# Residual of six tiles and attended half of four tiles: added by GpSimd's accumulating transfers in place of VectorE

## The chip, the cores and the metric

The kernel runs on one core of one Trainium2 chip. Its five engines are TensorE (PE; its weight loads are shown apart as PEld), VectorE (DVE), ScalarE (ACT), GpSimd (POOL) and SyncE (SP). Each works through its own list of instructions in order and waits on semaphores where it needs another engine or a transfer. Transfers between main memory and the on-chip memory (SBUF) are issued from an engine's queue and carried by 16 DMA engines. Matmul results are written to PSUM. The metric is the time of one execution in microseconds on the device.

## The reference

One layer of a bidirectional encoder, float32, S = 1024 tokens, width D = 1024, feed-forward width 2816:

```python
x = x + 0.5 * post1(FFN1(pre1(x)))
h = pre2(x); z = h @ w_in
x = x + post2(concat(attn, rwkv) @ w_out)     # h1 -> h2
x = x + 0.5 * post3(FFN2(pre3(x)))
```

`pre` and `post` are RMS norms with a gain. FFN is `(silu(h @ w_gate) * (h @ w_up)) @ w_down`. `attn` is a dilated attention of 8 heads (512 columns), `rwkv` a two-way RWKV-7 scan of 8 heads (512 columns). The change lies in the third line and in `pre3`. There, for each token, with `y` the concatenated 1024 columns:

```python
o  = y @ w_out
h2 = h1 + o / rms(o) * gain_post2
f  = h2 / rms(h2) * gain_pre3          # input of FFN2
```

## The kernel before, in words

The 1024 tokens are eight tiles of 128 rows, worked off in the order 2, 3, 4, 5 (half 0) and 0, 1, 6, 7 (half 1) of the token blocks. I call the tiles t0 to t7 in this working order. A row tile is 128 partitions by 1024 columns, 512 KB. In the rows of the instruction order below, t0 to t3 are `row_16320` to `row_16323`, and t4 to t7 are `row_16316` to `row_16319`.

Products are float32 made of two parts: every operand is split into a high part (ScalarE copy, L186) and a remainder (VectorE subtraction, L187), and a product is three matmuls (high x high, high x low, low x high). The feed-forward products use seven products for eight blocks (class `_GateUp`, n from 1 to 7). For this the weights' slabs and the rows are added and subtracted beforehand: the slabs by VectorE at L60 to L63, the rows by GpSimd in `factor_sums` (L339 to L343).

The stage of interest lies between the end of the RWKV part and FFN2. The attended part's product with its half of `w_out` was computed earlier and lies in main memory (`hp_d`). Then, for each tile, in `out_project` and `done`:

1. The tile's rows of `hp_d` are loaded into the row tile (SyncE).
2. For each 512 columns: 12 matmuls (L1064) of the RWKV half with `w_out` into a PSUM buffer `pw`, of which there are two, and a VectorE addition of `pw` to the row (L1095).
3. `post`: load of the tile's rows of `h1_d` into `res` (one buffer, SyncE, L182); sum of squares on ScalarE (L244), root (L245), reciprocal on VectorE (L246); the gain on VectorE (L256); the residual addition on VectorE (L257); store of the row to `h2_d` (SyncE, L258).
4. For the tile before: `pre`, that is the same three steps of the norm (L244 to L246) and the gain on VectorE (L266), in place in the row, so after the store of this tile. For tiles of half 1, `factor_sums` follows on GpSimd.
5. For the tile two back: `turn`, TensorE's transposes (L330) and the split of the result (L186, L187), the operand of FFN2's first products.

FFN2's first products (L81) run between these steps; the first slabs of their weights are loaded on GpSimd's queue and later ones on SyncE's (L284). A framework's scheduler fixes each engine's order when the program is built.

The row addition and the store stand in `post` so:

```python
nc.vector.scalar_tensor_tensor(ft, ft, rs, gb, op0=OP.mult, op1=OP.mult)   # L256
nc.vector.tensor_tensor(ft, ft, r, op=OP.add)                              # L257
self.nc.sync.dma_start(store[rows, :], ft)                                 # L258
```

Of the kernel before, what the change touches and what calls it, by code (L numbers as in the profile page):

```python
# [10 lines left out]
F32 = mybir.dt.float32  # L11
F32R = mybir.dt.float32r
AF = mybir.ActivationFunctionType
OP = mybir.AluOpType
# [4 lines left out]
S, D, DFF, INW = 1024, 1024, 2816, 3456  # L19
# [144 lines left out]
class _Kernel:  # L164
# [47 lines left out]
    def rstd(self, p, ss, n, scale, eps, post=1.0):  # L212
        V = self.nc.vector
        rs = p.tile([128, n], F32, name="rs", tag="rs", bufs=2)
        V.tensor_scalar(rs, ss, scale, eps, op0=OP.mult, op1=OP.add)
        self.nc.scalar.activation(rs, rs, AF.Sqrt)
        V.reciprocal(rs, rs)
        if post != 1.0:
            V.tensor_scalar(rs, rs, post, None, op0=OP.mult)
        return rs  # L220
# [25 lines left out]
        V.reciprocal(rs, rs)  # L246
        return rs

    def post(self, p, ft, t, gb, scale, res, store):

        nc = self.nc
        rows = slice(t * 128, (t + 1) * 128)
        r = p.tile([128, D], F32, name="res", tag="res")
        self.load(r, res[rows, :])
        rs = self.inv_rms(p, ft, scale)
        nc.vector.scalar_tensor_tensor(ft, ft, rs, gb, op0=OP.mult, op1=OP.mult)  # L256
        nc.vector.tensor_tensor(ft, ft, r, op=OP.add)  # L257
        self.nc.sync.dma_start(store[rows, :], ft)  # L258

    def pre(self, p, ft, gain=None):  # L260
# [825 lines left out]
    def out_project(self, psum, half, W, x, h2, done):  # L1086
        xh, xl = x[half]
        for i in range(4):
            t, ts = self.order[half * 4 + i], slice(i * 128, (i + 1) * 128)
            self.load(h2[t], self.hp_d[t * 128:(t + 1) * 128, :])  # L1090
            for dh in range(2):
                ps = psum.tile([128, 512], F32, name="pw", tag="d")
                self.out_products(ps, W, dh, xh, xl, ts)
                dst = h2[t][:, dh * 512:(dh + 1) * 512]
                self.nc.vector.tensor_tensor(dst, dst, ps, op=OP.add)  # L1095
            done(half * 4 + i)


# [64 lines left out]
    def run(self):  # L1163
        nc = self.nc
# [4 lines left out]
        with self.top as top:  # L1169
# [8 lines left out]
            with ExitStack() as st:  # L1178
                s_pg = ExitStack()
                pg, pt = self.pool(s_pg, "ps_g", space=PSUM), self.pool(s_pg, "ps_t", 2, space=PSUM)  # L1180
                rows = self.pool(st, "rows1", 8, **R)
# [4 lines left out]
                hand = self.pool(s_h0, "hand0", **R)  # L1186
# [30 lines left out]
                x2, low, ps = [], {}, {}  # L1217
                p = self.pool(st, "ffn1")
                hand = self.pool(st, "hand1")
                gb = self.row_bcast(hand, "ffn1_post_g")  # L1220
                LO = [12, 13, 14]

                def ready(half):
                    for ct in LO:
                        ps[ct, half] = self.product(psum, x2, low[ct], (half,))[0]

                def done(i, f):
                    if not i:
                        x2.extend(self.operand(xp, xp))
                    if i == 6:  # L1230
                        for ct in LO:
                            low[ct] = self.weights(ring, self.io["w_in"][0], INW, ATT + ct * 128, p, ("gh", "gl"), GB)
                    self.hand_over(hand, psum, f, i, natural, gb, 0.5, x0, self.h1_d, self.g2c, x2, ready)

                self.down(p, ring, rows, psum, self.hid_d[0], wd, self.ws_d[0], natural, done)
                x = x2
                vw = self.value_weights(ring)
# [80 lines left out]
            rows = self.pool(s_xn, "rows2", 8)  # L1318
            hr = self.row_tiles(rows)
            h2 = {t: hr[i] for i, t in enumerate(self.order)}  # L1320
# [15 lines left out]
            hand = self.pool(st, "hand2")  # L1336
            gb, late = self.row_bcast(hand, "mix_post_g"), {}
            f = self.factors(f0, None)

            def turn(i):  # L1340
                a, b = hr[i % 4], hr[i % 4 + 4]
                for n in (1, 2) if i < 4 else (3,):
                    self.turn_factor(pg, a, b, n, f, i % 4, "ge", 2)
                if i >= 4:
                    self.factor_sums(a, b, True)
# [4 lines left out]
                    self.factor_sums(hr[i - 4], hr[i])  # L1350

            def done(i):
                self.post(hand, hr[i], self.order[i], gb, 1.0, self.h1_d, self.h2_d)
                if i:
                    ready(i - 1)
                else:
                    late["gain"] = self.row_bcast(hand, "ffn2_pre_g")
                if i > 1:
                    turn(i - 2)

            for half in range(2):
                self.out_project(psum, half, W, x, h2, done)
# [10 lines left out]
            with ExitStack() as st:  # L1373
# [12 lines left out]
                p, hand = self.pool(st, "ffn2"), self.pool(st, "hand3")  # L1386
                gb = self.row_bcast(hand, "ffn2_post_g")
# [48 lines left out]
```

## Time and profile before

| | |
|---|---|
| median of 3 runs | 2369.25 us (2357.99 to 2371.84) |
| profiled execution, its own time | 2369.46 us |
| its span, first to last instruction | 2367.7 us |
| mean granted TensorE clock | 0.960 |
| busy: PE, PEld, DVE, ACT, POOL | 2212.2, 1784.9, 1782.8, 1034.4, 608.7 us |
| the stage of the change | about 1640 to 1752 us of the span |

Times inside the span are microseconds from its first instruction. In rows of the trace, `out<-in` are the program's names without buffer numbers: `row` a row tile, `pw` a PSUM buffer of the out-projection, `res` the residual rows, `d_h` the rows h1 or h2 in main memory, `d_hp` the attended half there, `raw` a slab of weights. "Idle before" is the time that the engine stood still ahead of an instruction, with what released it. The feed-forward products make up most of the span on TensorE; the stage above is about a twentieth of it.

### The profile page before, as it was taken

To read this page: it belongs to the slowest core of one execution; us is meant where nothing else is said; L and a number is where in the kernel's file an instruction comes from. 1 tells how busy PE (TensorE), PEld (TensorE's weight loads), DVE (VectorE), ACT (ScalarE), POOL (GpSimd) and SP (SyncE) were. 2 spreads that over 40 slices of the span, in tenths; PEclk is the share of its full clock that TensorE was granted. 3 is DMA by queue.
4 is the path that set the end of the run, shared out by engine and by line. 5 is a ranking of instruction groups with operands and counts; after the bars stand their busy time and mean duration, and the time that the engine had idled before them with its cause. 6 is when DMAs were issued, how large, how long until landed. Compare 5 with 4: busy or idle time off the path is not lost. (4 is left out here: it accounts for less than half of the span.)

```text
span 2367.7 us, 39507 instructions
## 1 busy us (share of the span) xinstructions
PE 2212.2 (93%) x14532; PEld 1784.9 (75%) x14532; DVE 1782.8 (75%) x2957; ACT 1034.4 (44%) x1958; POOL 608.7 (26%) x732
## 2 busy tenths in 40 slices
PE   6999999999999998999995889988799999999997
PEld 4788888878877676788774767765678888887886
DVE  8899999865676344667568767837889999987565
ACT  4322333354676413666545545445442333235453
POOL 6244443400000010111102242432334344441000
PEclk8999999999999998999996798989989999999999
DMA  5354445486652514322369676577534544447655
GB/s 156 107 174 151 170 146 170 167 266 193 220 185 98 193 42 134 91 81 71 94 161 223 165 183 176 151 208 256 178 95 168 174 167 154 169 153 265 195 188 181
DMA packets 359381, 386.04 MB, mean 163 GB/s; under 512 B 74258, under 2 KB 265618, under 8 KB 359188
## 3 DMA queue, kind: packets, MB, share of 16 engines
q1 hardware_dynamic: 308512, 276.43, 38.8%
q0 software_dynamic: 30320, 94.44, 11.3%
q10 hardware_dynamic: 20356, 12.66, 1.9%
q8 instruction: 114, 1.87, 0.3%
q14 instruction: 79, 0.65, 0.1%
HBM read 257.53 MB, written 125.89 MB: 162 GB/s over the span
## 5 line engine op out<-in xcount | busy, mean ns | idle before, releaser
L186 ACT ACTIVATE wh<-raw 128x512 fp32r<-128x512 f32 (+1 forms) x273 | 167.8, 626 | 264.1 <-DVE raw L62 95.0
L187 DVE TENSOR_TENSOR wl<-raw,wh 128x512 fp32r<-128x512 f32 (+1 forms) x273 | 277.6, 1020 | 3.1 <-ACT wh L186 2.0
L81 PE MATMUL gu<-xh,wh 128*128 128x512 f32 x704 | 277.9, 395 | 0.9 <-ACT xh L186 0.8
L81 PE MATMUL gu<-xl,wh 128*128 128x512 f32 x704 | 276.3, 393 | 0.0
L81 PE MATMUL gu<-xh,wl 128*128 128x512 f32 x704 | 276.2, 392 | 0.0
L415 PE MATMUL pd<-gl,gwh 128*128 128x512 f32 x616 | 240.4, 390 | 3.1 <-DVE gl L187 3.1
L415 PE MATMUL pd<-gh,gwh 128*128 128x512 f32 x616 | 239.6, 390 | 0.5 <-DVE row L86 0.5
L415 PE MATMUL pd<-gh,gwl 128*128 128x512 f32 x616 | 239.7, 389 | 0.0
L86 DVE TENSOR_TENSOR row<-gu,row 128x512 f32<-128x512 f32 x308 | 206.4, 682 | 23.2 <-PE gu L81 22.4
L187 DVE TENSOR_TENSOR gwl<-graw,gwh 128x512 fp32r<-128x512 f32 (+1 forms) x176 | 117.0, 667 | 129.7 <-ACT gwh L186 127.5
L116 POOL DMA_DIRECT2D d_hid<-row x154 | 84.7, 551 | 470.6 <-DVE row L114 444.2
L186 ACT ACTIVATE gwh<-graw 128x512 fp32r<-128x512 f32 (+1 forms) x176 | 101.4, 576 | 190.5 <-PE pd L415 162.2
L81 PEld LDWEIGHTS gu<-xh,wh 128*128 128x128 f32 x704 | 133.9, 190 | 29.5 <-ACT xh L186 2.0
L81 PEld LDWEIGHTS gu<-xl,wh 128*128 128x128 f32 x704 | 133.8, 190 | 27.9
L81 PEld LDWEIGHTS gu<-xh,wl 128*128 128x128 f32 x704 | 133.3, 189 | 27.5
L415 PEld LDWEIGHTS pd<-gl,gwh 128*128 128x128 f32 x616 | 115.6, 188 | 28.5 <-DVE gl L187 4.9
L415 PEld LDWEIGHTS pd<-gh,gwh 128*128 128x128 f32 x616 | 115.5, 188 | 25.6 <-DVE row L86 0.8
L415 PEld LDWEIGHTS pd<-gh,gwl 128*128 128x128 f32 x616 | 115.6, 188 | 23.8
L94 ACT ACTIVATE row<-row 128x512 f32<-128x512 f32 x44 | 27.9, 633 | 223.9 <-DVE row L86 216.4
L187 DVE TENSOR_TENSOR gl<-raw,gh 128x512 fp32r<-128x512 f32 x160 | 112.9, 717 | 15.7 <-ACT gh L186 15.4
L145 POOL TENSOR_TENSOR ws<-ws 128x512 f32<-128x512 f32 x88 | 114.4, 1300 | 1.2
L186 ACT ACTIVATE gh<-raw 128x512 fp32r<-128x512 f32 x160 | 98.0, 621 | 32.2 <-DMA raw<-in_ffn_w_down_dram 21.1
(356 smaller groups left out, 5353.4 us busy)
## 6 DMA issues: line engine op xcount, KB each, us to landing
d_hid<-row POOLq DMA_DIRECT2D x154, 256.0 KB, 2.5
graw<-d_hid SPq DMA_DIRECT2D x132, 256.0 KB, 3.0
raw<-in_ffn_w_gate_dram SPq DMA_DIRECT2D x88, 256.0 KB, 3.1
raw<-in_ffn_w_up_dram SPq DMA_DIRECT2D x88, 256.0 KB, 3.3
ws<-in_ffn_w_down_dram SPq DMA_DIRECT2D x88, 256.0 KB, 4.5
d_ws<-ws POOLq DMA_DIRECT2D x88, 256.0 KB, 2.3
raw<-d_ws SPq DMA_DIRECT2D x88, 256.0 KB, 2.7
raw<-in_ffn_w_down_dram SPq DMA_DIRECT2D x66, 256.0 KB, 3.3
```

The costliest lines, as they stand in the source:

```text
L81: self.K.nc.tensor.matmul(ps, a[:, k, :], b[:, k, :], start=(k == 0 and i == 0), stop=(k == 3 and i == 2))
L86: add = lambda o, x: V.tensor_tensor(o, ps, x, op=OP.add)
L94: A.activation(y[:, 0], y[:, 0], AF.Silu)
L116: put = lambda n, y: G.dma_start(self.hid[n - 1, j // 2], y)
L145: G.tensor_tensor(o, a, b, op=OP.subtract)
L186: self.nc.scalar.activation(h, src, AF.Copy)
L187: (eng or self.nc.vector).tensor_tensor(l, src, h, op=OP.subtract)
L415: T.matmul(ps[x], a[:, ts], b, start=(m == 0 and k == 0), stop=(m == NM - 1 and k == 2))
```

## The change

In half 0 (t0 to t3) the attended half is no longer loaded ahead. ScalarE copies `pw` into the row (L1104 of the new text, two copies per tile), and then one transfer from GpSimd's queue adds the tile's rows of `hp_d` to the row in SBUF (L1106, `accum_op` add, 512 KB). In half 1 the load and VectorE's additions stay (L1102).

In `post`, for the first six tiles (`fetch`), there is no load into `res`. After the gain (L257, before L256) a transfer from GpSimd's queue adds the tile's rows of `h1_d` to the row (L259), and the store follows (L262, before L258). t6 and t7 keep the load and the addition (L261, before L257). The gain of `pre` is L270, before L266.

So ten accumulating transfers are added on GpSimd's queue and eight copies on ScalarE; eight PSUM additions and six residual additions leave VectorE; four loads of `hp_d` and six of `h1_d` leave SyncE's queue.

```diff
-    def post(self, p, ft, t, gb, scale, res, store):
+    def post(self, p, ft, t, gb, scale, res, store, fetch=False):
...
-        r = p.tile([128, D], F32, name="res", tag="res")
-        self.load(r, res[rows, :])
+        if not fetch:
+            r = p.tile([128, D], F32, name="res", tag="res")
+            self.load(r, res[rows, :])
         rs = self.inv_rms(p, ft, scale)
         nc.vector.scalar_tensor_tensor(ft, ft, rs, gb, op0=OP.mult, op1=OP.mult)
-        nc.vector.tensor_tensor(ft, ft, r, op=OP.add)
+        if fetch:
+            nc.gpsimd.dma_start(ft, res[rows, :], accum_op=OP.add)
+        else:
+            nc.vector.tensor_tensor(ft, ft, r, op=OP.add)
         self.nc.sync.dma_start(store[rows, :], ft)
...
-            self.load(h2[t], self.hp_d[t * 128:(t + 1) * 128, :])
+            src = self.hp_d[t * 128:(t + 1) * 128, :]
+            if half:
+                self.load(h2[t], src)
             for dh in range(2):
                 ps = psum.tile([128, 512], F32, name="pw", tag="d")
                 self.out_products(ps, W, dh, xh, xl, ts)
                 dst = h2[t][:, dh * 512:(dh + 1) * 512]
-                self.nc.vector.tensor_tensor(dst, dst, ps, op=OP.add)
+                if half:
+                    self.nc.vector.tensor_tensor(dst, dst, ps, op=OP.add)
+                else:
+                    self.nc.scalar.copy(dst, ps)
+            if not half:
+                self.nc.gpsimd.dma_start(h2[t], src, accum_op=OP.add)
             done(half * 4 + i)
...
-                self.post(hand, hr[i], self.order[i], gb, 1.0, self.h1_d, self.h2_d)
+                self.post(hand, hr[i], self.order[i], gb, 1.0, self.h1_d, self.h2_d, i < 6)
```

The scheduler's order on the engines around the change follows, before and after, at three places. `junk` takes the squares that the sum is made of, `rs1` is the norm's factor, `wh` and `xh` are high parts and `wl` and `xl` remainders of weights and of the transposed rows.

First the start of the stage on ScalarE, before: the norms of t0 and t1, slab halves, the pre norm of t0, the norm of t2, and the first transposed rows.

```order
L244 ACTIVATE junk_16645,rs1_16646<-row_16320 128x1024
L245 ACTIVATE rs1_16646<-rs1_16646,eps0_69 128x1
L244 ACTIVATE junk_16686,rs1_16687<-row_16321 128x1024
L245 ACTIVATE rs1_16687<-rs1_16687,eps0_69 128x1
L186 ACTIVATE wh_16587<-raw_16585 128x512
L186 ACTIVATE wh_16593<-raw_16591 128x512
L186 ACTIVATE wh_16599<-raw_16597 128x512
L244 ACTIVATE junk_16694,rs1_16695<-row_16320 128x1024
L245 ACTIVATE rs1_16695<-rs1_16695,eps0_69 128x1
```

After, on ScalarE, from the norm of t1 to the norm of t2:

```order
L244 ACTIVATE junk_16682,rs1_16683<-row_16321 128x1024
L1104 COPY row_16322<-pw_16710 128x512
L245 ACTIVATE rs1_16683<-rs1_16683,eps0_69 128x1
L1104 COPY row_16323<-pw_16753 128x512
L244 ACTIVATE junk_16690,rs1_16691<-row_16320 128x1024
L186 ACTIVATE wh_16599<-raw_16597 128x512
L186 ACTIVATE wh_16605<-raw_16603 128x512
L245 ACTIVATE rs1_16691<-rs1_16691,eps0_69 128x1
L1104 COPY row_16323<-pw_16767 128x512
L244 ACTIVATE junk_16725,rs1_16726<-row_16322 128x1024
```

The last copy of t3 out of PSUM (`pw_16767`) now stands behind the pre norm's square of t0 (`junk_16690`). GpSimd's queue at the same place held four slab loads in a row before; after, it holds them between the transfers:

```order
L1106 DMA row_16320<-d_hp_83 128x1024
L288 DMA raw_16585<-in_ffn2_w_gate_dram 128x4x128
L288 DMA raw_16591<-in_ffn2_w_gate_dram 128x4x128
L1106 DMA row_16321<-d_hp_83 128x1024
L259 DMA row_16320<-d_h1_77 128x1024
L288 DMA raw_16597<-in_ffn2_w_gate_dram 128x4x128
L288 DMA raw_16603<-in_ffn2_w_gate_dram 128x4x128
L1106 DMA row_16322<-d_hp_83 128x1024
L259 DMA row_16321<-d_h1_77 128x1024
L1106 DMA row_16323<-d_hp_83 128x1024
L259 DMA row_16322<-d_h1_77 128x1024
```

Two slab loads have moved behind the residual transfer of t0; the residual transfers of t3, t4 and t5 follow.

Second, the middle of the stage on VectorE, before: the additions for t5 and t6 around the gain of pre of t3 (`b_ffn2_pre_g`) and the gain of post of t5 (`b_mix_post_g`).

```order
L1095 TENSOR_TENSOR row_16318<-row_16318,pw_16939 128x512
L266 SCALAR_TENSOR_TENSOR row_16323<-row_16323,rs1_16858,b_ffn2_pre_g_16653 128x1024
L246 RECIPROCAL rs1_16909<-rs1_16909 128x1
L256 SCALAR_TENSOR_TENSOR row_16317<-row_16317,rs1_16909,b_mix_post_g_16612 128x1024
L257 TENSOR_TENSOR row_16316<-row_16316,res_16847 128x1024
```

After, the same place on VectorE:

```order
L270 SCALAR_TENSOR_TENSOR row_16323<-row_16323,rs1_16848,b_ffn2_pre_g_16651 128x1024
L246 RECIPROCAL rs1_16897<-rs1_16897 128x1
L1102 TENSOR_TENSOR row_16318<-row_16318,pw_16927 128x512
L257 SCALAR_TENSOR_TENSOR row_16317<-row_16317,rs1_16897,b_mix_post_g_16612 128x1024
L187 TENSOR_TENSOR xl0_16310<-pt_16912,xh0_16309 128x4x128
```

The gain of t5 stands behind the gain of pre of t3 in both; the residual addition is gone, and the first addition of t6 has come behind the gain of pre.

Third, the end of the stage on VectorE, before: from the last addition of t7 (`row_16319`). The gain of pre of t7 stands another seven rows below.

```order
L1095 TENSOR_TENSOR row_16319<-row_16319,pw_17009 128x512
L246 RECIPROCAL rs1_16978<-rs1_16978 128x1
L246 RECIPROCAL rs1_17026<-rs1_17026 128x1
L256 SCALAR_TENSOR_TENSOR row_16319<-row_16319,rs1_17026,b_mix_post_g_16612 128x1024
L266 SCALAR_TENSOR_TENSOR row_16317<-row_16317,rs1_16978,b_ffn2_pre_g_16653 128x1024
L257 TENSOR_TENSOR row_16318<-row_16318,res_16967 128x1024
L187 TENSOR_TENSOR xl1_16312<-pt_17041,xh1_16311 128x4x128
L246 RECIPROCAL rs1_17034<-rs1_17034 128x1
L187 TENSOR_TENSOR xl1_16312<-pt_17128,xh1_16311 128x4x128
L266 SCALAR_TENSOR_TENSOR row_16318<-row_16318,rs1_17034,b_ffn2_pre_g_16653 128x1024
L257 TENSOR_TENSOR row_16319<-row_16319,res_17023 128x1024
```

After, on VectorE, from the residual addition of t6 to the gain of pre of t7:

```order
L261 TENSOR_TENSOR row_16318<-row_16318,res_16955 128x1024
L270 SCALAR_TENSOR_TENSOR row_16317<-row_16317,rs1_16966,b_ffn2_pre_g_16651 128x1024
L1102 TENSOR_TENSOR row_16319<-row_16319,pw_16997 128x512
L187 TENSOR_TENSOR xl1_16312<-pt_17029,xh1_16311 128x4x128
L246 RECIPROCAL rs1_17014<-rs1_17014 128x1
L257 SCALAR_TENSOR_TENSOR row_16319<-row_16319,rs1_17014,b_mix_post_g_16612 128x1024
L246 RECIPROCAL rs1_17022<-rs1_17022 128x1
L261 TENSOR_TENSOR row_16319<-row_16319,res_17011 128x1024
L270 SCALAR_TENSOR_TENSOR row_16318<-row_16318,rs1_17022,b_ffn2_pre_g_16651 128x1024
L246 RECIPROCAL rs1_17039<-rs1_17039 128x1
L187 TENSOR_TENSOR xl1_16312<-pt_17072,xh1_16311 128x4x128
L270 SCALAR_TENSOR_TENSOR row_16319<-row_16319,rs1_17039,b_ffn2_pre_g_16651 128x1024
```

The residual addition of t6 and the gain of pre of t5 now stand ahead of the last addition of t7. On SyncE's queue at this end, the load of t7's residual, five loads of FFN2's slabs and then the store of t7 came one after the other before; after, these rows are:

```order
L262 DMA d_h2_80<-row_16318 128x1024
L182 DMA res_17011<-d_h1_77 128x1024
L262 DMA d_h2_80<-row_16319 128x1024
L288 DMA raw_17167<-in_ffn2_w_gate_dram 128x4x128
L288 DMA raw_17169<-in_ffn2_w_gate_dram 128x4x128
L288 DMA raw_17171<-in_ffn2_w_up_dram 128x4x128
```

The store of t7 now stands ahead of these slab loads.

## The prediction

> **What bounds the kernel now.** I read the chain that ended last first, to see which engine sets the end, and then the stage that the diff touches by itself.
>
> ```profile
> PE 26%; DVE 2%; issue 1%; DMA 1%; ACT 0%; POOL 0%; SPq 0%; DVEq 0%; POOLq 0%
> PE gu L81 17%; PE pd L415 9%; DVE row L266 0%; DVE row L257 0%; DMA d_h<-row 0%; DVE row L256 0%; PE pt L330 0%; ACT junk L244 0%; DMA raw<-in_ffn_w_gate_dram 0%; DMA res<-d_h 0%; DVE row L86 0%; POOL row L339 0%; DVE wl L187 0%; POOL row L340 0%; DVE raw L61 0%
> ```
>
> The end hangs on TensorE's products. The lines of this change (L256, L257, L266, the store into d_h) are on the chain, each with under half a per cent. VectorE's busy time over the whole span therefore says little; the stage must be read by itself, in slices of 20 us:
>
> ```profile
> 1640.00:1660.00 20.00, 19.31 (x89) 15.53 (x89) 14.76 (x24) 10.60 (x22) 1.50 (x2) 1.00 0.75 253
> 1660.00:1680.00 20.00, 17.85 (x90) 14.38 (x89) 19.36 (x29) 12.15 (x25) 0.00 (x0) 1.00 0.49 169
> 1680.00:1700.00 20.00, 18.49 (x86) 14.68 (x85) 17.10 (x22) 9.09 (x19) 6.90 (x4) 1.00 0.45 150
> 1700.00:1720.00 20.00, 7.10 (x36) 5.34 (x36) 14.19 (x18) 6.60 (x13) 14.58 (x10) 0.72 0.61 185
> ```
>
> After the slice and its length stand the busy times of PE, PEld, DVE, ACT and POOL, the granted clock, the DMA share and GB/s. Up to 1700 TensorE works 18 to 19 of 20 us with VectorE nearly as full; in the last slice it works 7.1. The chain inside the stage, in order of time:
>
> ```profile
> 1672.00 2.88 DMA d_h<-row
> 1674.97 1.28 DVE row L266
> ...
> 1685.61 3.05 DMA d_h<-row
> 1688.75 1.28 DVE row L266
> ...
> 1694.81 1.16 ACT junk L244 x2
> ...
> 1697.36 0.30 ACT rs L245
> 1697.69 0.17 DVE rs L246
> ...
> 1752.35 147.83 PE gu L81 x652
> ```
>
> VectorE and the store take turns here: the gain of pre (L266) overwrites the row in place, so it waits until the store has read it. Two tiles pass between 1674.97 and 1688.75, 6.9 us each. From 1752.35 on TensorE's work has no gap: the total moves by as much as that point moves.
>
> **What is removed.** Eight PSUM additions and six residual additions leave VectorE:
>
> ```profile
> L1095 DVE TENSOR_TENSOR row<-row,pw x16: 665/675/689, 1640.2 to 1695.3; 128x512 f32<-128x512 f32 x16
> L257 DVE TENSOR_TENSOR row<-row,res x8: 1212/1218/2308, 1656.3 to 1707.7; 128x1024 f32<-128x1024 f32 x8
> DMA to landing us min/median/max: 4.2/4.7/8.3
> ```
>
> That is 8 x 0.675 + 6 x 1.218 = 12.7 us of VectorE, but the stage cannot gain as much, since TensorE is close behind:
>
> ```profile
> 1646.25 0.39 PE L1064 MATMUL pw<-woh,xh 128*128 128x512 f32 x1
> ...
> 1651.71 0.39 PE L1064 MATMUL pw<-woh,xh 128*128 128x512 f32 x1
> ...
> 1703.72 1.03 PE L330 MATMUL pt<-ident,row 128*128 128x128 f32 x8
> ```
>
> Between those two starts lie 24 steps, 5.46 us: the 24 matmuls of one tile. With its eight transposes (1.03) TensorE needs 6.5 us per tile against 6.9 now. The ten loads that leave SyncE's queue were issued ahead of their use; they cost the path nothing, except that `res` has one buffer, which holds up the last tiles (below).
>
> **What is added.** Eight ScalarE copies out of PSUM, and ten accumulating transfers of 512 KB on GpSimd's queue. The copies I price by one of the same size out of PSUM:
>
> ```profile
> L186 ACT ACTIVATE xh<-pt 128x512 fp32r<-128x512 f32 x15 | 8.4, 597 | 21.4 <-PE pt L330 21.4
> ```
>
> 8 x 0.6 = 4.8 us beside 9 to 12 of 20 us of ScalarE's own work: the engine has room, and only their place in its order counts. The accumulates are another matter. What was an addition beside a load issued early becomes a transfer that starts when the row is ready, and the next step waits for its landing. I call the time from issue to landing L. The trace has no such operation; the nearest are these of the window 1636 to 1715, with the median time to landing last:
>
> ```profile
> res<-d_h SPq DMA_DIRECT2D x8, 512.0 KB, 4.7
> d_h<-row SPq DMA_DIRECT2D x8, 512.0 KB, 3.0
> raw<-in_ffn_w_gate_dram POOLq DMA_DIRECT2D x4, 256.0 KB, 4.2
> ```
>
> Lower end of L: a load of the same rows in this stage, median 4.7; the same bytes must come, and the addition might be free. Upper end: the slowest such load, 8.3, and a store of 3.0 behind it, 11.3. I take 4.7 + 3.0 = 7.7, as the row is read, added to and written; for the first two, which fall into the slice with a DMA share of 0.75, I take 8.3, the load that was issued there.
>
> How often does L stand on the path? ScalarE's copy of t3's second half stands behind the square of t0's pre norm, which waits for t0's residual. So the path is: copies of t0; its attended half (L); norm 1.16 + 0.30 + 0.17 = 1.63; gain L257, 1.28; residual (L); on ScalarE the square, two weight halves (priced as the copy) and the root, 1.16 + 2 x 0.60 + 0.30 = 2.66; copy of t3, 0.60; its attended half (L), norm 1.63, gain 1.28, residual (L), store 2.88; L270 of t3, 1.28; gain of t5, 1.28, which stands behind it on VectorE; residual of t5 (L), store 3.05, L270 of t5, 1.28. Behind that stands the last PSUM addition of t7. The fixed parts are 1.63 + 1.28 + 2.66 + 0.60 + 1.63 + 1.28 + 2.88 + 1.28 + 1.28 + 3.05 + 1.28 = 18.9 us, and five L come to 2 x 8.3 + 3 x 7.7 = 39.7. The two weight halves wait for slab loads that GpSimd now issues behind t0's residual; these land in 4.2 us, before the residual does, so they add nothing. Where the path starts and what follows it, by VectorE's and SyncE's rows:
>
> ```profile
> 1645.98 0.69 DVE L1095 TENSOR_TENSOR row<-row,pw 128x512 f32<-128x512 f32 x1 [0.22 <-PE pw L1064]
> ...
> 1650.56 0.69 DVE L1095 TENSOR_TENSOR row<-row,pw 128x512 f32<-128x512 f32 x1
> ...
> 1695.30 0.67 DVE L1095 TENSOR_TENSOR row<-row,pw 128x512 f32<-128x512 f32 x1
> ...
> 1716.01 1.28 DVE L266 SCALAR_TENSOR_TENSOR row<-row,rs,b_ffn_pre_g 128x1024 f32<-128x1024 f32 x1
> 1702.49 1.80 SPq L284 DMA_DIRECT2D raw<-in_ffn_w_gate_dram  x2
> ```
>
> The first is t0's second addition; a copy in its place ends at 1646.6. The second is t1's, begun when its products were done. Then t7's last addition, now at 1695.30, comes at 1646.6 + 18.9 + 39.7 = 1705.2: **9.9 us later**. With L at 4.7 the path gives 1689.0, but TensorE is not there before 1650.5 + 6 x 6.5 = 1689.5, six tiles after t1, so 5.8 us earlier at best. With L at 11.3 it is 1722.0, 26.7 later.
>
> **What comes back behind it.** Today the last L266 starts 20.7 us after t7's addition, since the residual load of t7 waits for the one buffer. With only t6 and t7 loaded, what is left is 0.67 + 1.63 + 1.28 + 1.22 + 3.05 and handovers, some 8.3 us: 12.4 less. But FFN2's first products also wait for its weight slabs, whose loads begin at 1702.49, 7.2 us after that addition; in the new order on SyncE they stand behind t7's store, 0.67 + 1.63 + 1.28 + 1.22 = 4.8 and some 0.7 of handing over and issuing after it, so they come 1.7 earlier. And VectorE, which then builds the sums of these slabs, has t5's L266 (1.28) and t6's residual (1.22) behind it before the last addition. I take 1.7 + 2.5 = **4.2 us back**, between nothing (another load holds the slabs) and 12.4.
>
> Net 9.9 - 4.2 = 5.7 us on the profiled execution's 2369.46: 2375.2, so 2375. That execution is within 0.3 us of the median of the three runs (2369.25), so nothing is to be shifted. The edit breaks even where five L come to 34.0, 6.8 each.
>
> **A rule that speaks against it.** GpSimd issues the transfers while VectorE runs:
>
> ```profile
> 1654.86 0.75 POOL L284 DMA_DIRECT2D raw<-in_ffn_w_gate_dram  x1 [16.09 <-DVE wl L187]
> L116 POOL DMA_DIRECT2D d_hid<-row x154 | 84.7, 551 | 470.6 <-DVE row L114 444.2
> ```
>
> An issue in this stage took 0.75 against a mean of 0.55 over 154 issues in FFN stages where VectorE works too: a fifth of a microsecond more. The Trainium skill's page "SBUF — State Buffer", section "A bandwidth-pool intuition that's wrong (but worth ruling out)", says that a transfer issued by GpSimd can wait until VectorE releases a port that they share, 620 ns alone becoming some 3100. By that rule each of five transfers would take up to 2.5 us more, an estimate from that page; the rows here speak against it.
>
> **The rivals.**
> - An accumulate costs what a load costs (L = 4.7). For it: the addition needs no engine. Against it: reading and writing the row is more than a load does. 5.8 earlier and 4.2 back: 10.0 less, 2359.5. Chance 0.18.
> - Each issue on GpSimd waits for the VectorE operation in progress, at most the longest in the rows above, 2.3 us (L257). Five of these on the path: 11.5 more, 2386.7. The 0.75 row is against it. Chance 0.10.
> - The other side: the accumulate is slow itself, or the 16 engines choke on it. The stage already holds them for 0.75, 0.49 and 0.45 of three slices. One 512 KB copy holds them 1.5 us (524 KB at 169 / 0.49 = 345 GB/s). With the slowest load, the store and one more pass, 8.3 + 3.0 + 1.5 = 12.8, five L are 64.0 and t7's addition 34.2 late; less 4.2, 30.0: 2399.5. It decides from L = 11.5 on, where the loss passes 1% (23.7 us). Then ScalarE's copies wait behind squares, two PSUM buffers stay full, and TensorE starves. Chance 0.22.
> - The change does not do what it says: the order shows the additions gone from VectorE and the transfers on GpSimd, so 0.02.
>
> **How the numbers follow.** My forecast has 0.48. One per cent is about what a measurement of this kernel tells from no change. The range takes the cheap rival's 2359 and the slow one's 2400. Faster by over 1% would need 23.7 us from a stage whose floor gives 5.8 + 12.4: 0.02. Slower by over 1% is the slow rival and a piece of the forecast's upper bound (11.3): 0.24. Within: 0.74.
>
> **What would show it.** Time to landing of the accumulates: near 7.7, or 4.7, or over 11. The last PSUM addition of t7 near 1705, then the last gain of pre about 8 us later. TensorE idle on PSUM buffers released by ScalarE's copies between 1660 and 1700. GpSimd's accumulate issues at 0.55 to 0.75 or above 2. The unbroken L81 stretch beginning near 1758. The forecast is wrong if L is not near 7.7, or if t0's norm is not what holds t3's copy.

## The result, and the profile after

The changed kernel took 2375.94 us, median of 17 runs (2368.25 to 2390.03), beside 2369.25 us for the kernel before in as many runs on the same chip. The ratio is 1.0037 with a 95% interval of 1.0020 to 1.0054: slower by 8.8 us, between 4.7 and 12.8 (the two medians lie 6.7 apart), so clear of no change at all, and inside the 1% that the prediction called no change. Measured again ("the change again" below) it was 1.0041 (1.0015 to 1.0068). The profiled execution after took 2372.87 us, its span is 2370.5 us.

The two spans differ by only 2.8 us, less than the runs do. A part of the program that the change does not touch hides the rest: the last matmul of the attended projection, well ahead of the stage, began some 11 us earlier in the profile after (1552.8 against 1563.8). The granted clock between 1200 and 1400 was 0.85 there instead of 0.80, which I take for the reason. So I compare stages from a mark inside the stage: the second half of t0 leaving PSUM (1645.98 before, by VectorE; 1637.65 after, by ScalarE's copy). From there to the span's end it is 721.7 us before and 732.9 after: 11.1 us more.

The stage in slices of 20 us after, columns as before; on this scale the stage lies 8.3 us earlier than in the slices before (1645.98 less 1637.65), so the slices compare only roughly:

```profile
1640.00:1660.00 20.00, 16.51 (x73) 13.37 (x72) 7.37 (x12) 9.88 (x20) 6.19 (x8) 1.00 1.01 269
1660.00:1680.00 20.00, 13.46 (x59) 10.29 (x58) 9.87 (x17) 9.41 (x20) 2.56 (x3) 0.91 0.96 260
1680.00:1700.00 20.00, 16.91 (x82) 12.97 (x80) 15.04 (x24) 9.97 (x23) 6.45 (x5) 1.00 0.68 155
1700.00:1720.00 20.00, 12.07 (x63) 9.34 (x61) 15.23 (x16) 7.37 (x15) 15.91 (x11) 0.98 0.46 144
```

VectorE is now idle half the time up to 1680 (7.4 and 9.9 of 20 us, 14.8 and 19.4 before), and TensorE with it: 13.5 us where it worked 17.9. The DMA engines are full (1.01 and 0.96; the share adds up the time of all packets, so it can pass 1), at hardly more bytes in the first slice than before (269 against 253 GB/s). In the last slice TensorE does more (12.1 against 7.1).

The ten transfers on GpSimd's queue, by line, with the time from issue to landing below each:

```profile
L259 POOL DMA_DIRECT2D row<-d_h x6: 850/852/877, 1649.4 to 1690.6; - x6
DMA to landing us min/median/max: 6.5/7.4/9.6
L1106 POOL DMA_DIRECT2D row<-d_hp x4: 855/910/967, 1638.5 to 1661.5; - x4
DMA to landing us min/median/max: 7.5/8.3/9.9
```

The path to t7's last addition, by the rows of three engines. First GpSimd (t0's attended half, t0's residual, t3's attended half, then the residuals of t3 and t5):

```profile
1638.55 0.97 POOL L1106 DMA_DIRECT2D row<-d_hp  x1 [9.70 <-ACT row L1104]
...
1649.40 0.88 POOL L259 DMA_DIRECT2D row<-d_h  x1 [3.19 <-DVE row L257]
...
1661.53 0.85 POOL L1106 DMA_DIRECT2D row<-d_hp  x1 [2.69 <-ACT row L1104]
...
1677.44 0.85 POOL L259 DMA_DIRECT2D row<-d_h  x1 [8.25 <-DVE row L257]
...
1690.62 0.85 POOL L259 DMA_DIRECT2D row<-d_h  x1 [5.61 <-DVE row L257]
```

Then, on ScalarE, t0's mark, the squares that wait for the transfers, and the copy of t3 that stands behind the second square:

```profile
1637.65 0.58 ACT L1104 COPY row<-pw 128x512 f32<-128x512 f32 x1
...
1646.11 1.06 ACT L244 ACTIVATE junk<-row 128x1024 f32<-128x1024 f32 x1 [1.12 <-DMA row<-d_hp]
...
1657.53 1.06 ACT L244 ACTIVATE junk<-row 128x1024 f32<-128x1024 f32 x1 [0.90 <-DMA row<-d_h]
...
1660.67 0.57 ACT L1104 COPY row<-pw 128x512 f32<-128x512 f32 x1
...
1671.50 1.06 ACT L244 ACTIVATE junk<-row 128x1024 f32<-128x1024 f32 x1 [2.38 <-DMA row<-d_hp]
```

And VectorE, from t3's gain of post to t7's last addition and its gain of pre:

```profile
1675.63 1.28 DVE L257 SCALAR_TENSOR_TENSOR row<-row,rs,b_mix_post_g 128x1024 f32<-128x1024 f32 x1
...
1687.20 1.27 DVE L270 SCALAR_TENSOR_TENSOR row<-row,rs,b_ffn_pre_g 128x1024 f32<-128x1024 f32 x1
...
1700.94 2.28 DVE L270 SCALAR_TENSOR_TENSOR row<-row,rs,b_ffn_pre_g 128x1024 f32<-128x1024 f32 x1
1703.15 0.67 DVE L1102 TENSOR_TENSOR row<-row,pw 128x512 f32<-128x512 f32 x1
...
1713.90 1.77 DVE L270 SCALAR_TENSOR_TENSOR row<-row,rs,b_ffn_pre_g 128x1024 f32<-128x1024 f32 x1
```

The last two landings of the path, and TensorE's stretch at its end, in the chain that ended last:

```profile
1677.44 6.54 DMA row<-d_h
...
1690.62 6.63 DMA row<-d_h
...
1754.74 24.60 PE gu L81 x108
```

This is the path that the prediction drew. From t0's mark to t7's last addition it takes 1703.15 - 1637.65 = 65.5 us, against 1695.30 - 1645.98 = 49.3 before: 16.2 us later. Behind it the last gain of pre comes after 10.8 us instead of 20.7. TensorE's unbroken stretch begins at 1754.74, that is 117.1 us from the mark against 106.4 before (1752.35): 10.7 us later, nearly all of the 11.1.

### The profile page after: what moved, and what is told of

It reads as the page before. It is cut to its first block, busy times and chain, and to the rows that moved or that the text cites. A ratio compares the mean times of both kernels' runs of the same rounds, so it can differ in the third digit from the quotient of the medians.

```text
span 2370.5 us, 39507 instructions
## 1 busy us (share of the span) xinstructions
PE 2217.0 (94%) x14532; PEld 1788.3 (75%) x14532; DVE 1769.6 (75%) x2943; ACT 1037.4 (44%) x1966; POOL 616.2 (26%) x742
## 5 line engine op out<-in xcount | busy, mean ns | idle before, releaser
L81 PE MATMUL gu<-xh,wh 128*128 128x512 f32 x704 | 277.2, 394 | 2.2 <-ACT wh L186 1.2
L187 DVE TENSOR_TENSOR wl<-raw,wh 128x512 fp32r<-128x512 f32 (+1 forms) x273 | 272.7, 1002 | 4.8 <-ACT wh L186 3.8
L81 PE MATMUL gu<-xh,wl 128*128 128x512 f32 x704 | 275.7, 392 | 0.0
L81 PE MATMUL gu<-xl,wh 128*128 128x512 f32 x704 | 275.6, 392 | 0.0
L81 PEld LDWEIGHTS gu<-xh,wh 128*128 128x128 f32 x704 | 133.4, 190 | 31.5 <-ACT xh L186 2.0
L81 PEld LDWEIGHTS gu<-xl,wh 128*128 128x128 f32 x704 | 133.4, 189 | 27.6
L81 PEld LDWEIGHTS gu<-xh,wl 128*128 128x128 f32 x704 | 133.0, 189 | 27.6
```

Source lines behind the costliest of these rows:

```text
L81: self.K.nc.tensor.matmul(ps, a[:, k, :], b[:, k, :], start=(k == 0 and i == 0), stop=(k == 3 and i == 2))
L187: (eng or self.nc.vector).tensor_tensor(l, src, h, op=OP.subtract)
```

## The experiments

The question was which part costs the 8.8 us, and whether it is landings in series, the load on the DMA engines, or ScalarE's copies. The table gives for each run the ratio to the kernel before with its interval, and from its profile how many of the eight gains of pre VectorE does ahead of t7's last PSUM addition, and three times: from t0's mark to that addition, from there to the last gain of pre, and from t0's mark to the end of the span.

| run | ratio to before | gains ahead | t0 to t7's addition | to the last gain | t0 to the end |
|---|---|---|---|---|---|
| before | 1 | 5 | 49.3 | 20.7 | 721.7 |
| the change | 1.0037 (1.0020 to 1.0054) | 6 | 65.5 | 10.8 | 732.9 |
| the change again | 1.0041 (1.0015 to 1.0068) | 6 | 66.6 | 10.7 | 733.5 |
| residuals alone | 1.0001 (0.9983 to 1.0020) | 6 | 58.4 | 10.7 | 725.1 |
| attended half alone | 1.0055 (1.0035 to 1.0074) | 4 | 55.5 | 27.0 | 736.6 |
| attended half, two residual buffers | 1.0008 (0.9984 to 1.0032) | 5 | 58.9 | 12.4 | 728.1 |
| plain loads | 1.0001 (0.9985 to 1.0017) | 6 | 55.6 | 11.4 | 724.6 |
| copies by VectorE | 1.0054 (1.0031 to 1.0078) | 5 | 63.8 | 14.2 | 735.8 |
| copies alone | 1.0019 (0.9999 to 1.0039) | 4 | 45.9 | 26.7 | 727.4 |
| residuals twice | 1.0131 (1.0102 to 1.0161) | 3 | 65.4 | 34.0 | 752.5 |
| before, two residual buffers | 0.9977 (0.9951 to 1.0003) | 5 | 47.0 | 12.4 | 716.2 |
| the same again | 0.9979 (0.9956 to 1.0003) | 5 | 47.9 | 12.4 | 717.2 |
| and the stores on GpSimd's queue | 1.0010 (0.9991 to 1.0030) | 5 | 51.7 | 14.4 | 721.8 |
| two buffers, residuals added by GpSimd | 1.0003 (0.9979 to 1.0027) | 6 | 54.5 | 10.8 | 723.9 |

A thousandth is 2.4 us. The last column follows the ratios roughly; a single profile, and there is only one of the kernel before, can be off by 4 or 5 us.

The scheduler orders each build anew. Where more gains of pre stand ahead of t7's last addition, that addition comes later and less is left behind it, so the second time and the third are not the same piece of work in every run. Only their sum, from t0's mark to the last gain, can be compared between builds with different numbers of gains ahead: 70.0 us before, 76.3 in the change.

### Residuals alone

The change without its half 0 part: the attended half of all tiles is loaded ahead and added by VectorE.

```diff
-            src = self.hp_d[t * 128:(t + 1) * 128, :]
-            if half:
-                self.load(h2[t], src)
+            self.load(h2[t], self.hp_d[t * 128:(t + 1) * 128, :])
...
-                if half:
-                    self.nc.vector.tensor_tensor(dst, dst, ps, op=OP.add)
-                else:
-                    self.nc.scalar.copy(dst, ps)
-            if not half:
-                self.nc.gpsimd.dma_start(h2[t], src, accum_op=OP.add)
+                self.nc.vector.tensor_tensor(dst, dst, ps, op=OP.add)
```

> Only the six residuals are added by accumulating transfers; the attended half of t0 to t3 is loaded ahead and added by VectorE, as before the change. Theory (transfers in series on the path): from t1's gain only three landings are left before t7's last addition, 3 x 7.4 = 22.2 us, with 15.1 us of stores and gains between them, so that addition comes about 1692 on the scale of the profile before, 3 us earlier than before, and 4 to 5 us more come back behind it: 2361 to 2366 us, faster than before. Rival (every transfer costs its share of the loss, by its traffic): six tenths of 6.7 us, 2373.

It came out level with before; the interval, -4.0 to 4.7 us, takes in the near end of the theory and just the rival. The expected place was wrong: t7's addition came 9.1 us later than before instead of 3 earlier, and 10.0 us less passed behind it; one more gain of pre stands ahead of it than before. The landings were short (median 5.9), but the stores behind two of them were not: in this run's chain

```profile
1647.86 7.34 DMA row<-d_h
...
1655.21 4.90 DMA d_h<-row
...
1669.45 6.17 DMA row<-d_h
...
1675.67 5.88 DMA d_h<-row
```

a store takes 4.9 and 5.9 us, where the prediction's path had 2.88 and 3.05. Six residual transfers cost nothing in sum against the kernel before: from t0's mark to the last gain it is 69.2 us against 70.0. But that kernel waits at its end for its one residual buffer, and this one doesn't.

### The attended half alone

The change without its residual part.

```diff
-                self.post(hand, hr[i], self.order[i], gb, 1.0, self.h1_d, self.h2_d, i < 6)
+                self.post(hand, hr[i], self.order[i], gb, 1.0, self.h1_d, self.h2_d)
```

> Only the attended half of t0 to t3 is added by accumulating transfers behind ScalarE's copies; all eight residuals are loaded and added by VectorE, as before the change. Theory: two landings in series (t1, then t3), and t3's gain of pre comes no later than before, so nothing is lost: 2365 to 2370 us. Rival A (shares by traffic): four tenths of 6.7 us, 2372. Rival B (the loss is TensorE waiting for ScalarE's copies, 7 us in the profile of the change): 2376.

13 us slower (8.3 to 17.5), which is more than the 8.8 (4.7 to 12.8) of the whole change, though the intervals overlap. The theory's "two landings in series" was wrong, as the rows of its GpSimd show:

```profile
1639.18 0.97 POOL L1106 DMA_DIRECT2D row<-d_hp  x1 [9.22 <-ACT row L1104]
...
1645.93 0.92 POOL L1106 DMA_DIRECT2D row<-d_hp  x1 [4.22 <-ACT row L1104]
...
1657.01 0.90 POOL L1106 DMA_DIRECT2D row<-d_hp  x1 [5.06 <-ACT rs L245]
1666.46 0.86 POOL L1106 DMA_DIRECT2D row<-d_hp  x1 [8.54 <-ACT rs L245]
```

and of its ScalarE:

```profile
1664.54 1.06 ACT L244 ACTIVATE junk<-row 128x1024 f32<-128x1024 f32 x1 [4.89 <-DMA row<-d_hp]
...
1665.60 0.56 ACT L1104 COPY row<-pw 128x512 f32<-128x512 f32 x1
```

Each tile's last copy stands on ScalarE behind the square of the tile before, which waits for its landing; so the attended halves of t1, t2 and t3 land one after the other. That makes t7's addition 6.2 us late, although one gain of pre fewer stands ahead of it than before. As much comes on behind it: 27.0 us to the last gain instead of 20.7, with that one gain more to do. The next run asks how much of it is the one buffer. Rival B's 7 us were one wait counted twice, on TensorE (3.5) and on its weight load (3.9).

### The attended half with two residual buffers

Against the change:

```diff
-    def post(self, p, ft, t, gb, scale, res, store, fetch=False):
+    def post(self, p, ft, t, gb, scale, res, store, fetch=False, bufs=1):
...
-            r = p.tile([128, D], F32, name="res", tag="res")
+            r = p.tile([128, D], F32, name="res", tag="res", bufs=bufs)
...
-                self.post(hand, hr[i], self.order[i], gb, 1.0, self.h1_d, self.h2_d, i < 6)
+                self.post(hand, hr[i], self.order[i], gb, 1.0, self.h1_d, self.h2_d, False, 2)
```

> The run with the attended half alone, with two buffers for the residual rows. In that run's profile t7's last addition came 5.0 us later than before, counted from the end of the RWKV stage's last matmul, and the gain of pre of t7 another 6.3 us later behind it. Theory (the 6.3 come from the one residual buffer, whose loads were pushed back in turn): with two buffers the gain of t7 starts 10 to 13 us after its last addition instead of 27, and of the 13 us over before some 5 to 7 remain. Rival (VectorE's or the slabs' work holds the end): 11 to 14 over before, as with one buffer.

Of the 13 us, 1.9 are left (-3.8 to 7.6), and the last gain comes 12.4 us behind t7's addition. The rival is out: the one buffer does hold up the end of the attended half's run. Its residual loads are pushed back tile by tile, each behind the addition of the tile before. The change does not show that loss, as it loads only t6's and t7's residual. But a second buffer also gives the kernel before some 5 us (below), with as many gains ahead and the same 12.4 us. Against that kernel the attended half still costs about 7 us (0 to 14), and its last gain comes 71.3 us from t0's mark instead of 59.4 and 60.2. So the landings have a price of their own here, beside the buffer.

### Plain loads in place of accumulating ones

```diff
-            nc.gpsimd.dma_start(ft, res[rows, :], accum_op=OP.add)
+            nc.gpsimd.dma_start(ft, res[rows, :])
...
-                self.nc.gpsimd.dma_start(h2[t], src, accum_op=OP.add)
+                self.nc.gpsimd.dma_start(h2[t], src)
```

> The ten transfers stay on GpSimd's queue at the same places with the same waits, but are plain loads: they overwrite the row and leave both additions out. Theory (an accumulate takes a load and a write-back, 7.4 to 8.3 us, a plain load 4.7): time to landing of the ten falls to about 5, each of five on the path gives back about 3 us: 2360 us. Rival (the landing is a fixed cost of a transfer on this queue at this place, whether it adds or not): landing stays above 7 us and the time at 2374 to 2376.

Level with before, so 8 to 9 us under the change. The landings are 5.5 (residual) and 5.9 (attended half), not 4.7, so there is no gain over before. By these medians the five landings on the path fall by 2 x 2.4 + 3 x 1.9 = 10.5 us; t7's addition, behind six gains in all three, comes 9.9 and 11.0 us earlier than in the two profiles of the change: the path shortens by what the landings shorten. This is the run that shows the cause: the same transfers at the same places, and without the adding the loss is gone. The residuals' row of this run:

```profile
L259 POOL DMA_DIRECT2D row<-d_h x6: 528/528/549, 1644.3 to 1677.8; - x6
```

The issue itself takes 0.53 us here and 0.85 in the change. What an accumulate takes more, the queue's own share of the 16 DMA engines shows between 1636 and 1720 (packets, MB, share). Before, with four slab loads on this queue:

```profile
q0 software_dynamic: 320, 1.05, 4.6%
```

The change:

```profile
q0 software_dynamic: 1760, 6.29, 39.6%
```

The plain loads:

```profile
q0 software_dynamic: 1760, 6.29, 21.8%
```

For the same packets and bytes, ten transfers take (39.6 - 4.6)% x 84 us = 29.4 us of all engines when they add, and (21.8 - 4.6)% x 84 = 14.4 when they don't: 2.9 us against 1.4 each, twice the time, if the four slab loads take in both what they took before. The Trainium skill's page "Collectives: The Full Stack", section "The bandwidth ceiling: the fold count and why AG ≠ RS ≠ AR", says that the reduce step of a collective runs at half the rate of a copy, since the add needs two source reads. The factor of the transfers here agrees, 2.0; that the second read is the reason, no run here shows.

### Copies by VectorE

```diff
-                    self.nc.scalar.copy(dst, ps)
+                    self.nc.vector.tensor_copy(dst, ps)
```

> All as in the change, but VectorE instead of ScalarE copies the out-projection of t0 to t3 out of PSUM; ScalarE's squares, which wait for the transfers, then no longer stand ahead of these copies. Rival (ScalarE's order is the whole loss): back to the time before, within 2 us. Theory (landings in series, whichever engine holds the copies): behind VectorE's gains the path is still attended half of t1, residual of t1, store, gain of pre of t1, gain of t3, residual of t3, residual of t5, that is four landings of 7.4 to 8.3, and little is gained: 5 to 9 us above before.

12.8 us above before (7.3 to 18.5): not better than the change, and more than expected, though the interval reaches into the 5 to 9. The rival is out: that the copies wait on ScalarE is not the whole loss. On VectorE they wait as well, behind its gains, and in this run's chain the transfer of t3's attended half, issued right behind two others, takes longer to land than any in the change:

```profile
1664.12 13.56 DMA row<-d_hp
```

### Copies alone

The run with the attended half alone, without its four transfers, so the attended half of t0 to t3 is left out.

```diff
-            if not half:
-                self.nc.gpsimd.dma_start(h2[t], src, accum_op=OP.add)
```

> As the run with the attended half alone, but without its four transfers: ScalarE copies the out-projection of t0 to t3 into the rows, nothing is added to it (the attended half of these four tiles is left out), and all residuals are loaded and added by VectorE. Theory (the landings cost, not the copies): before, or up to 4 us faster. Rival (TensorE waits for ScalarE's copies, transfers or not): 8 to 13 us above before, as with the transfers.

4.5 us above before, with an interval that just reaches no change (-0.2 to 9.2): between the two expectations. t7's addition comes 3.4 us earlier, with four gains of pre ahead of it instead of five, and the last gain 26.7 us behind it, as with the transfers; from t0's mark to the last gain it is 72.6 us against 70.0. In SyncE's and VectorE's rows

```profile
1694.34 0.42 SPq L182 DMA_DIRECT2D res<-d_h  x1
1700.12 1.21 DVE L261 TENSOR_TENSOR row<-row,res 128x1024 f32<-128x1024 f32 x1
```

t7's residual is loaded only at 1694.34, 13 us after its last PSUM addition (1680.95), and added when it has landed 5.8 us later. Removing work ahead of the one residual buffer only lengthens the wait for it. Why the end is then later than before, and not equal, stays open. So a part of the attended half's 13 us may come from the copies and the new order, and not from the landings.

### Residuals twice

Each of the six residuals is added twice, by two transfers in a row.

```diff
             nc.gpsimd.dma_start(ft, res[rows, :], accum_op=OP.add)
+            nc.gpsimd.dma_start(ft, res[rows, :], accum_op=OP.add)
```

> All as in the change, but each of the six residual transfers is issued twice in a row, so that the residual of six tiles is added twice. Theory (landings in series: the residuals of t0, t3 and t5 are on the path): three more landings of 7.4 and their issues, 20 to 25 us above the change, some 30 above before. Rival (the loss is the load on the 16 DMA engines): 3 MB more, 6 x 3 us of traffic in a stage that is half idle after its first third: 5 us above the change or less.

31 us above before (24 to 38), as landings in series gave, and far from the 12 to 14 that the load on the DMA engines would have given. The place was another than expected: t7's addition came no later than in the change (65.4 us), with only three gains of pre ahead of it here, and the last gain 34.0 us behind it. GpSimd issues in order, and the second transfer of a tile waits for the landing of the first, by GpSimd's waits in this run five times and 23.4 us in all,

```profile
POOL row L260 <- DMA row<-d_h: 23.4, 5, 6.7
```

so the later residuals were held up on that queue. That the number came out as expected is therefore partly luck; what holds is that waiting for landings costs far more than the bytes do.

### Two residual buffers in the kernel before, with two variants

The prediction held that the one buffer delays the end. The edit is that of the attended half's run, in the kernel before:

> The kernel before with two buffers for the residual rows in this stage, all else as before (the order then puts t7's store ahead of FFN2's slab loads on SyncE). Theory (the one buffer delays t6's and t7's residual additions, and what the change gives back behind t7's addition is this): the last gain of pre starts about 8 instead of 20.7 us after t7's last addition, 4 to 5 us come through to the end: 2365 us. Rival (FFN2's slab loads hold the end of the stage anyway): 2369.

> The kernel before with two residual buffers once more, since the first interval just reached no change: theory 3 to 6 us below before; rival: no difference from before within 2 us.

5.4 and 5.0 us below before, each interval just reaching no change. Weighted by their widths the two give 0.9978, with a 95% interval of some 0.9961 to 0.9995. The last gain comes 12.4 us behind t7's addition instead of 20.7 (8 was expected), with five gains ahead of it in both: this is what the one buffer costs. It is the only kernel here that is faster than both, by about 5 and 14 us.

To let FFN2's slab loads go ahead of the last store, the stores went to GpSimd's queue:

```diff
-        self.nc.sync.dma_start(store[rows, :], ft)
+        (nc.gpsimd if bufs == 2 else nc.sync).dma_start(store[rows, :], ft)
```

> The kernel before with two residual buffers, and the stores of h2 in this stage on GpSimd's queue, so that FFN2's slab loads on SyncE's queue no longer stand behind the last store. Theory (what two buffers give at the end is cut short by the slab loads behind t7's store): 3 to 5 us faster than with two buffers alone, so 7 to 10 below before. Rival (the slabs do not hold the end, or GpSimd's factor sums are delayed by the stores' waits): as with two buffers alone, 3 to 5 below before, or nothing.

Nothing is left of the gain. The slab loads did come off the store, and stopped at something else; SyncE's waits between 1680 and 1730:

```profile
SPq L284 <- PE gu L81: 22.1, 1, 22.1
```

The second slab's load waits 22.1 us for the first products (L81), which still read the buffer that it goes into.

And the additions taken off VectorE without any transfer, t0's to t4's residual added by GpSimd:

```diff
...
-        nc.vector.tensor_tensor(ft, ft, r, op=OP.add)
+        (nc.gpsimd if pool else nc.vector).tensor_tensor(ft, ft, r, op=OP.add)
...
-                self.post(hand, hr[i], self.order[i], gb, 1.0, self.h1_d, self.h2_d, 2)
+                self.post(hand, hr[i], self.order[i], gb, 1.0, self.h1_d, self.h2_d, 2, i < 5)
```

> The kernel before with two residual buffers, and the residual additions of the first five tiles done by GpSimd's own additions instead of VectorE's; nothing else moved off. Theory (taking additions off VectorE helps if the next step waits for no transfer: TensorE needs 6.5 us per tile against 6.9): t7's last addition 2 to 4 us earlier than before, and 6 to 9 us below before in all. Rival (GpSimd's addition takes about twice VectorE's 1.22 us, and VectorE's operations beside it are stretched from 1.3 to 2.2 us): the pace stays, before or slower.

No gain either (0.7 us above before, -5.0 to 6.4), and nothing seen of the 5 us of two buffers. By this run's rows for the two lines,

```profile
L257 POOL TENSOR_TENSOR row<-row,res x5: 2370/2396/3368, 1643.5 to 1671.3; 128x1024 f32<-128x1024 f32 x5
L266 DVE SCALAR_TENSOR_TENSOR row<-row,rs,b_ffn_pre_g x8: 1272/1278/3023, 1652.6 to 1698.7; 128x1024 f32<-128x1024 f32 x8
```

GpSimd's addition takes 2.4 us, twice VectorE's, and a gain of VectorE's is stretched to 3.0.

### The change again

> The change itself once more, for a second profile and a narrower time: from the last matmul of the attended projection to the end 812 to 818 us against 803.7 before, and 6 to 12 us above before. A rival on the size: the first profile's stage was unlucky, and 806 to 810 us come now.

9.7 us above before (3.6 to 16.1). From the start of the last matmul of the attended projection to the end it took 811.3 us, just below what was expected, against 817.7 in the first profile. The difference of 6.4 us lies ahead of t0's mark; from that mark on the two agree within 0.7 us. There the median landings were 8.5 (attended half) and 7.8 (residual).

## Why the prediction was right, and which terms were off

**The bound.** Right. The total moved with the point at which TensorE's stretch begins (10.7 us later from t0's mark, the end 11.1), and VectorE's 12.7 us gave nothing: VectorE's busy time fell by 13.2 us over the span (1782.8 to 1769.6), and the kernel became slower.

**The landing time.** Right in size. 8.3 was taken for the first two and 7.7 for the others; the medians are 8.3 (attended half) and 7.4 (residual). On the path the five were 7.6, 8.1, 10.0, 6.5 and 6.6 us by the rows above (from issue to the square that follows, and in the chain for the last two), 38.8 in sum against 39.7. That the adding makes the landing long is shown by the plain loads. But the size was put together otherwise than it came out: 4.7 for a load and 3.0 for a store were added, where a plain load at these places took 5.5 to 5.9 and the adding 1.9 to 2.4 more. That the sum fits so well is partly luck.

**The path.** Right in its order, and the rows carry its main steps. Mis-sized in the term "fixed parts, 18.9": between the end of t0's copy (1638.2) and 1703.15 lie 64.9 us; less the 38.8 of the landings that is 26.1, so 7.2 more. The largest piece is t3's norm: 4.1 us from landing to gain (1671.50 to 1675.63) instead of 1.63, since ScalarE and VectorE had two transposed halves and t1's gain of pre ahead of it. The rest is 0.3 us from each finished row to the issue on GpSimd (four or five times), an addition or a residual in front of two gains, and the last gain at 2.28 instead of 1.28 beside GpSimd's sums. The statement that the two weight halves add nothing was also off: their slab loads landed 8.3 us after issue in the crowded slice, not 4.2, and held the copy of t3 for 0.6 us.

**t7's last addition.** 9.9 us later was forecast; from t0's mark it is 16.2 and 17.3 us. In the first profile the difference of 6.3 is the 7.2 of the fixed parts, less 0.9 by which the landings were shorter.

**What comes back.** 4.2 us was forecast; the addition is 16.2 and 17.3 late, the end 11.1 and 11.8, so 5.1 and 5.5 come back. That the last gain would come soon behind t7's addition was right: 10.8 us (8.3 was forecast, 20.7 before). How much the one buffer holds back is shown by the two runs with two buffers, 20.7 to 12.4. The slab part was wrong, 0.8 us lost where 1.7 were to come back: the slab loads began 8.0 us after t7's addition, not 5.5, and behind the first of them the next waited for a buffer. The 2.5 us for VectorE's two operations were not measured apart. So that the whole of 4.2 came near is luck in part. And the last gain is only 6.2 us later than before from t0's mark, where the end is 11.1 later: some 5 us more are lost between the last gain and TensorE's stretch, and by what stays open. SyncE's row after:

```profile
1711.10 4.03 SPq L288 DMA_DIRECT2D raw<-in_ffn_w_gate_dram  x2
```

**The sum.** 5.7 us was forecast. The runs say 8.8 (4.7 to 12.8) and 9.7 (3.6 to 16.1), the profiles 11.1 and 11.8. So the direction and the mechanism hold, but the net was too small by 3 to 6 us: by the first profile 6 us too little ahead of t7's addition, 1 us too little behind it. That 2375 lies within 1 us of the median of 2375.94 is luck.

**The rivals.** That an accumulate costs what a load costs is out (2.9 against 1.4 us of the engines, and 8 to 9 us of the total). That TensorE starves behind ScalarE's copies happened once, for 3.5 us. That GpSimd's issues wait for VectorE is out: the six residual issues took 0.850 to 0.877 us each, where plain loads take 0.528; the third of a microsecond goes with the adding, and nothing like 2.3 is seen. The rule of the Trainium skill's page "SBUF — State Buffer", weighed in the prediction, does not show in these rows; its figures are for a VectorE copy, and here VectorE ran additions and gains. The slow accumulate would have needed 11.5 us, which no accumulate in the two profiles of the change reaches (at most 10.2).

**What I had not seen.** How much of the comparison is the one buffer of the kernel before. Against that kernel the residuals alone cost nothing, the attended half alone 13 us, both together 9; with these intervals it can't be told whether the halves add up. Against the kernel with two buffers, which has that buffer twice, they cost about 5, 7 and 14 to 15 us by the ratios of the table, each uncertain by some 5 to 7. There the residual transfers have a price too, and the halves add up within the noise. So the change hides a part of its own price, since it also takes away the wait for the buffer.

## What to carry to other kernels

An addition moved from an engine into a transfer is not taken off the path when the next step needs its result: count the landings that stand in series, at twice a load's share of the DMA engines, before counting the engine time saved. Look first at what the last tiles wait for; a second buffer for the residual rows gave about 5 us, where none of the ways of taking additions off VectorE gave anything over before. Compare profiles from a mark inside the stage: here an untouched stretch ahead of it differed by 11 us between two profiles and hid most of the loss. And look at what stands ahead of such a mark in each build: t7's last addition had three to six gains of pre ahead of it.

## What the runs showed of the hardware that was not expected

A 512 KB accumulating transfer takes 0.85 us to issue on GpSimd against 0.53 for the plain one, and holds the 16 DMA engines 2.9 us against 1.4. With six of them in the stage the median landing was 5.9 us, with ten 7.4 to 8.5. Other loads suffer with them: those of half 1's attended half on SyncE's queue, in the change between 1636 and 1720,

```profile
row<-d_hp SPq DMA_DIRECT2D x4, 512.0 KB, 11.2
```

landed in 11.2 us. With plain loads on GpSimd's queue in place of the accumulating ones they landed in 6.9:

```profile
row<-d_hp SPq DMA_DIRECT2D x4, 512.0 KB, 6.9
```
